# Two plain pairs and a later norm at the head of the squared-relu stages

## The chip, the core and the metric

The kernel runs on one core of a Trainium2 chip. The metric is the device time of one execution, in microseconds (us); less is better. Every execution computes the whole function from inputs in device memory.

## What is computed

Three blocks follow each other on a sequence of 512 tokens with 16 meta tokens in front (528 in all) and a width of 1024: a hybrid layer (gated DeltaNet and short convolution, then a gated MLP), a block of sparse attention, and a block of attention with forget gates ("Fox"). The last two blocks each end with the stage that is changed here. All arithmetic is float32; `w1` of the stage is 1024 x 4096, `w2` 4096 x 1024, `DEPTH_2` is 2.

```python
def rms_norm(x, g):
    xf = x.astype(jnp.float32)
    y = xf * lax.rsqrt(jnp.mean(xf * xf, axis=-1, keepdims=True) + EPS)
    return (y * g.astype(jnp.float32)).astype(x.dtype)

def sq_relu_mlp(x, w1, w2):
    h = jax.nn.relu(x @ w1)
    return (h * h) @ w2
...
    for i in range(DEPTH_2):
        hn = rms_norm(h, attn_norm[i])
...
        h = h + sq_relu_mlp(rms_norm(h, mlp_norm[i]), mlp_w1[i], mlp_w2[i])
    return h[:, N_META:N_META + S]
```

## The kernel before

Activations lie transposed: `h` has 8 tiles of 128 channels by 528 tokens. A float32 product is made of three fp32r matmuls: every operand is split into a high part (ScalarE copies it to fp32r, `xh`, `wh`) and a low part (VectorE subtracts, `xl`, `wl`), and hi x hi, hi x lo and lo x hi are added in PSUM. `products` (line 100) does this for a weight tile of 128 columns that `weight_parts` has split (L83 on ScalarE, L84 on VectorE); weights come through a ring `wr` of three buffers filled by DMAs of the SP queue.

`mlp` runs twice: stage 0 behind the sparse attention on all 528 tokens (halves of 264), stage 1 behind Fox on the last 512 (halves of 256). Its first matrix is cut in 4 chunks of 4 pairs of column tiles. Each pair is multiplied with `seven`, a scheme with seven products of half-size blocks in place of eight: 84 matmuls a pair. For that the weights of a pair are added in four steps (L119 and L120 on VectorE, L121 and L122 on GpSimd) and split (L128, L129); the products are L136. `Squares` combines the results, takes relu and square, and splits them into `fh` and `fl` (L190, L191). After each chunk `down` multiplies with the second matrix (L1032), and `add` multiplies the result by `rrow`, the squared norm factor of each token (L1576), and adds it to `h` (L1577). The channel gains of the norm are in the operands already (`k.par(norm, i)`), the factor of a token comes last, since relu and square let it through as its square.

The token side of `seven` needs seven operands: with the tokens in halves a and b and the channels in halves 1 and 2, these are b11, b21, b22 (scaled parts of `h`) and t1 to t4 (sums of two to four of them). `combined` makes all seven for each of the four channel tiles q, each split in a high part (L1526 or L190) and a low part (L1527 or L191), while `before` still runs the attention's last output projection (L100, residual added at L941). The tiles `xh`/`xl` hold b11, b21, b22 and t3, the tiles `bigh`/`bigl` hold t1, t2 and t4. With `late=True` the first call of `seven` takes the products of b11, b22 and b21 first.

After the second pair, `token_rsqrt` makes the norm's factors: ScalarE squares `h` (L246), GpSimd adds the squares (L247), TensorE sums over channels (L255), VectorE makes the inverse root in a chain of small operations on `rcol` (L215 to L222), TensorE turns `rcol` into a row by five transposes (L266), and L1588 squares it.

The order of instructions on each engine isn't written by hand: the kernel is built with a scheduler that simulates the program and places each operation as its operands and buffers come free. So a change in the code of a stage can move its operations well past those of their neighbours. PSUM has eight banks in one ring (`pd`).

Of the kernel before, what the change touches and what calls it, by code (L numbers as in the profile page):

```python
# [15 lines left out]
D = 1024  # L16
# [30 lines left out]
class K:  # L47
# [56 lines left out]
    def seven(self, wdram, x, n, evac, late=False):  # L104
# [36 lines left out]
        def bank():  # L141
            return self.pst("pd")[:, :half]
# [7 lines left out]
        x1, z = bank(), None  # L150
# [3 lines left out]
        if late:  # L154

            weights(2)
            z = bank()
            product(z, q["s4"], "b22")
            product(x1, q["12"], "b21", start=False)
            evac.out11(x1)  # L160
            weights(1)
        u, y, v = bank(), bank(), bank()
        if late:
            product(y, q["s3"], "t3")
            product(v, q["s1"], "t1")
        product(u, q["s2"], "t2")
        evac.second(u)
        if not late:
            weights(1)
            product(y, q["s3"], "t3")  # L170
            product(v, q["s1"], "t1")
        evac.third(v)
        if not late:
            weights(2)
            product(x1, q["12"], "b21", start=False)
            evac.out11(x1)
        evac.out22(y)
        if not late:
            z = bank()
            product(z, q["s4"], "b22")  # L180
# [1334 lines left out]
def combined(k, h, x, norm, lo, n, pool):  # L1515

    nc = k.nc
    m = n // 2
    a, b = slice(lo, lo + m), slice(lo + m, lo + n)

    def put(name, i, v, scale=None):
        hi, lw = (t[:, i, :m] for t in x[name])
        if scale is None:
            k.split(hi, lw, v)
        else:
            nc.scalar.activation(hi, v, AF.Copy, scale=scale)  # L1526
            nc.vector.scalar_tensor_tensor(lw, v, scale, hi, ALU.mult, ALU.subtract)  # L1527

    for i in range(4):
        p, q = k.par(norm, i), k.par(norm, i + 4)  # L1530
        put("b11", i, h[:, i, a], p)
        put("b21", i, h[:, i + 4, a], q)
        g22 = pool.tile([128, T // 2], F32, name="g22", tag="fh", bufs=RING)[:, :m]
        nc.scalar.activation(g22, h[:, i + 4, b], AF.Copy, scale=q)
        put("b22", i, g22)
        g12 = pool.tile([128, T // 2], F32, name="g12", tag="fh", bufs=RING)[:, :m]
        nc.scalar.activation(g12, h[:, i, b], AF.Copy, scale=p)
        t = pool.tile([128, T // 2], F32, name="gt", tag="fl", bufs=RING)[:, :m]
        nc.vector.tensor_tensor(t, g22, g12, ALU.subtract)
        put("t3", i, t)  # L1540
        t = pool.tile([128, T // 2], F32, name="gt", tag="fl", bufs=RING)[:, :m]
        nc.vector.scalar_tensor_tensor(t, h[:, i, a], p, g12, ALU.mult, ALU.subtract)
        put("t1", i, t)
        nc.vector.tensor_tensor(g22, g22, t, ALU.add)
        put("t2", i, g22, -1.0)
        nc.vector.scalar_tensor_tensor(t, h[:, i + 4, a], q, g22, ALU.mult, ALU.subtract)
        put("t4", i, t, -1.0)


def mlp(k, io, h, i, before, lo=0, n=T):  # L1550
# [3 lines left out]
    w1, w2 = io["wm1"], io["wm2"]  # L1554
    with (
# [6 lines left out]
        pairs = [t[:, 2 * c : 2 * c + 2].rearrange("p a t -> p (a t)").rearrange("p (q t) -> p q t", q=4)  # L1562
                 for t in k.operand2() for c in range(4)]
        x = dict(zip(("b11", "b21", "b22", "t3"), zip(pairs[:4], pairs[4:])))
# [6 lines left out]
        def add(j):  # L1571
# [6 lines left out]

            return ev

        norm = []
# [461 lines left out]
```

## Time and profile before

| | us |
|---|---|
| three runs, median (lowest, highest) | 2635.54 (2629.37, 2642.49) |
| the profiled run, its time | 2630.84 |
| its span | 2629.1 |
| TensorE matmul busy | 2500.4 (95%), 18396 matmuls |
| VectorE busy | 1772.3 (67%) |
| ScalarE busy | 1189.7 (45%) |
| GpSimd busy | 549.3 (21%) |
| mean granted TensorE clock | 0.976 of full |

A busy TensorE isn't yet a TensorE at its peak: a matmul at half clock is busy twice as long. The shares are means over many stages, so the rows further below are taken by stages. In rows of the trace, PE is TensorE's matmuls, PEld its weight loads, DVE VectorE, ACT ScalarE, POOL GpSimd and SPq the queue that issues the DMAs. Lines are those of the kernel before.

### The profile page before, as it was taken

The page shows a single profiled execution, that of the slowest core. Times are in us where ns is not written, and L with a number is a line of the kernel's source. Part 1 is how long each engine was busy: PE and PEld are TensorE (multiplying, and loading weights), DVE is VectorE, ACT ScalarE, POOL GpSimd, SP SyncE. Part 2 cuts the span into 40 slices and gives each one's busy share as a digit, 9 for nine tenths or more (in the row PEclk, how much of TensorE's full clock was granted, in tenths as well). Part 3 has the DMA queues.
Part 4 walks back from the last instruction along what each step waited for, and adds up shares of the span by engine and source line. Part 5 has one row for each costly group of instructions (what it writes and reads, how often), then busy time and mean ns, then how long its engine had stood idle before and what let it go on. Part 6 is the DMA issues. An engine that isn't in the chain of part 4 may idle for free. (4 is left out here: it accounts for less than half of the span.)

```text
span 2629.1 us, 47488 instructions
## 1 busy us (share of the span) xinstructions
PE 2500.4 (95%) x18396; PEld 2315.7 (88%) x18396; DVE 1772.3 (67%) x3698; ACT 1189.7 (45%) x2439; POOL 549.3 (21%) x663
## 2 busy tenths in 40 slices
PE   8899999999999999999869979999999999799999
PEld 8888999999899888888868979999999988688987
DVE  7878788666554444336998496676755777866764
ACT  5434445353423222334447553453535766535533
POOL 2322213100002111013641031121213443211210
PEclk9999999999999999999989989999999989899999
DMA  4334332524562333333321222332433322233322
GB/s 153 92 94 120 84 95 90 118 88 131 171 207 89 96 92 94 96 89 110 83 66 47 72 79 92 105 101 78 129 98 88 90 66 64 66 94 108 105 81 96
DMA packets 148434, 257.32 MB, mean 98 GB/s; under 512 B 66560, under 2 KB 70688, under 8 KB 148208
## 3 DMA queue, kind: packets, MB, share of 16 engines
q1 hardware_dynamic: 91392, 236.47, 29.5%
q10 hardware_dynamic: 56816, 17.82, 3.5%
q8 instruction: 145, 2.38, 0.4%
q14 instruction: 81, 0.66, 0.1%
HBM read 223.39 MB, written 22.34 MB: 93 GB/s over the span
## 5 line engine op out<-in xcount | busy, mean ns | idle before, releaser
L100 PE MATMUL ps_pd<-bigh,wh 128*128 128x256 f32 (+5 forms) x2256 | 693.5, 309 | 16.7 <-ACT bigh L193 6.2
L100 PE MATMUL ps_pd<-bigh,wl 128*128 128x256 f32 (+5 forms) x2256 | 691.4, 308 | 10.5 <-DVE wl L84 10.5
L100 PE MATMUL ps_pd<-bigl,wh 128*128 128x256 f32 (+5 forms) x2256 | 690.6, 307 | 1.8 <-DVE bigl L194 1.5
L83 ACT ACTIVATE wh<-wr 128x1024 fp32r<-128x1024 f32 (+3 forms) x303 | 311.3, 1028 | 657.5 <-PE ps_pd L100 262.0
L100 PEld LDWEIGHTS ps_pd<-bigh,wh 128*128 128x128 f32 (+1 forms) x2256 | 429.5, 191 | 38.0 <-ACT bigh L193 6.2
L100 PEld LDWEIGHTS ps_pd<-bigh,wl 128*128 128x128 f32 (+1 forms) x2256 | 429.6, 191 | 29.9 <-DVE wl L84 12.8
L84 DVE TENSOR_TENSOR wl<-wr,wh 128x1024 fp32r<-128x1024 f32 (+3 forms) x291 | 352.0, 1210 | 152.7 <-ACT wh L83 145.0
L100 PEld LDWEIGHTS ps_pd<-bigl,wh 128*128 128x128 f32 (+1 forms) x2256 | 429.3, 190 | 21.1 <-DVE bigl L194 3.8
L1032 PE MATMUL ps_pd<-fh,wh 128*128 128x264 f32 (+1 forms) x944 | 311.8, 335 | 2.1 <-ACT wh L83 2.1
L1032 PE MATMUL ps_pd<-fl,wh 128*128 128x264 f32 (+1 forms) x944 | 313.5, 334 | 0.0
L1032 PE MATMUL ps_pd<-fh,wl 128*128 128x264 f32 (+1 forms) x944 | 312.1, 335 | 0.5 <-DVE wl L84 0.5
L1032 PEld LDWEIGHTS ps_pd<-fh,wh 128*128 128x128 f32 x944 | 176.2, 188 | 23.1 <-ACT wh L83 4.2
L1032 PEld LDWEIGHTS ps_pd<-fh,wl 128*128 128x128 f32 x944 | 176.7, 188 | 20.0 <-DVE wl L84 1.0
L1032 PEld LDWEIGHTS ps_pd<-fl,wh 128*128 128x128 f32 x944 | 177.1, 188 | 19.1
L128 ACT ACTIVATE wh<-wr 128x1024 fp32r<-128x1024 f32 (+1 forms) x128 | 119.7, 949 | 147.6 <-PE ps_pd L1032 51.2
L129 DVE TENSOR_TENSOR wl<-wr,wh 128x1024 fp32r<-128x1024 f32 (+1 forms) x128 | 154.4, 1219 | 12.3 <-ACT wh L128 11.3
L136 PE MATMUL ps_pd<-xh,wl 128*128 128x264 f32 (+1 forms) x512 | 148.2, 292 | 6.6 <-DVE wl L129 6.4
L136 PE MATMUL ps_pd<-xh,wh 128*128 128x264 f32 (+1 forms) x512 | 149.5, 293 | 3.4 <-ACT wh L128 1.8
L136 PE MATMUL ps_pd<-xl,wh 128*128 128x264 f32 (+1 forms) x512 | 149.0, 291 | 3.4 <-DVE xl L191 2.1
L121 POOL TENSOR_TENSOR wr<-wr 128x512 f32<-128x512 f32 x32 | 51.3, 1602 | 449.8 <-DMA wr<-wm 175.7
L247 POOL TENSOR_TENSOR acc<-acc,sq 128x512 f32<-128x512 f32 (+1 forms) x35 | 60.7, 1735 | 300.4 <-ACT sq L246 300.1
L1576 DVE TENSOR_TENSOR y<-ps_pd,rrow 128x264 f32<-128x264 f32 (+1 forms) x96 | 49.1, 515 | 100.8 <-PE ps_pd L1032 100.7
(501 smaller groups left out, 5527.3 us busy)
## 6 DMA issues: line engine op xcount, KB each, us to landing
wr<-w SPq DMA_DIRECT2D x72, 512.0 KB
wr<-wm SPq DMA_DIRECT2D x128, 256.0 KB
wr<-wm SPq DMA_DIRECT2D x64, 512.0 KB
wr<-wgu SPq DMA_DIRECT2D x44, 512.0 KB
wr<-wa SPq DMA_DIRECT2D x17, 512.0 KB
wr<-wkv SPq DMA_DIRECT2D x17, 512.0 KB
wr<-wdn SPq DMA_DIRECT2D x16, 512.0 KB
wr<-wao SPq DMA_DIRECT2D x16, 512.0 KB
```

The lines of the kernel that those rows point to most:

```text
L83: nc.scalar.activation(wh, wr, AF.Copy)
L84: (self.low or nc.vector).tensor_tensor(wl, wr, wh, ALU.subtract)
L100: nc.tensor.matmul(ps[:, :half], a[:, k], b[k][:, ts], start=(k == 0 and i == 0), stop=(k == kt - 1 and i == 2))
L121: nc.gpsimd.tensor_tensor(g1[:, 1], g2[:, 0], g4[:, 0], ALU.add)
L128: nc.scalar.activation(wh[:, : 4 * m], v, AF.Copy)
L129: nc.vector.tensor_tensor(wl[:, : 4 * m], v, wh[:, : 4 * m], ALU.subtract)
L136: nc.tensor.matmul(ps, a[:, q], c[:, q], start=(start and q == 0 and i == 0), stop=(q == 3 and i == 2), skip_group_check=not start,)
L247: (eng or nc.vector).tensor_tensor(acc, acc, sq, ALU.add)
L1032: nc.tensor.matmul(pss[h][:, :half], a[:, q], b[f0 + q][:, ts], start=(f0 + q == 0 and i == 0), stop=(f0 + q == nf - 1 and i == 2),)
L1576: nc.vector.tensor_tensor(y, ps, rs[:, t], ALU.mult)
```

## The change

The first two pairs of a stage's first chunk (`PLAIN = 2`) are no longer multiplied with `seven` but by `plain`: two weight tiles of 128 columns each, 96 matmuls a pair at L100, with relu, square and split behind each. So the token tiles are now split whole: `xh` and `xl` hold all eight tiles of scaled `h` in 528 (512) columns, and b11, b21, b12 and b22 are views of them. `combined` is replaced by `operand_sums`, which makes t1 to t4 for one channel tile, and is called for two of them behind each plain pair; t3 moves to `bigh`/`bigl`. `seven` loses its `late` order. The squares for the norm are issued behind the first pair that `seven` multiplies, the chain on `rcol` at the end of chunk 0, where `rcol` is squared while it is small, and the five transposes stand in the first call of `add`, at the first result of `down`.

```diff
-    def seven(self, wdram, x, n, evac, late=False):
+    def seven(self, wdram, x, n, evac):
...
-def combined(k, h, x, norm, lo, n, pool):
+def operand_sums(k, h, x, norm, lo, n, i, pool):
...
-    for i in range(4):
-        p, q = k.par(norm, i), k.par(norm, i + 4)
-        put("b11", i, h[:, i, a], p)
-        put("b21", i, h[:, i + 4, a], q)
-        g22 = pool.tile([128, T // 2], F32, name="g22", tag="fh", bufs=RING)[:, :m]
-        nc.scalar.activation(g22, h[:, i + 4, b], AF.Copy, scale=q)
-        put("b22", i, g22)
...
+    g22 = pool.tile([128, T // 2], F32, name="g22", tag="fh", bufs=RING)[:, :m]
+    nc.scalar.activation(g22, h[:, i + 4, b], AF.Copy, scale=q)
+    g12 = pool.tile([128, T // 2], F32, name="g12", tag="fh", bufs=RING)[:, :m]
+    nc.scalar.activation(g12, h[:, i, b], AF.Copy, scale=p)
+    t = pool.tile([128, T // 2], F32, name="gt", tag="fl", bufs=RING)[:, :m]
+    nc.vector.tensor_tensor(t, g22, g12, ALU.subtract)
+    put("t3", t)
...
-        combined(k, h, x, f"mnorm{i}", lo, n, s)
+        for c in (0, 4, 1, 5, 2, 6, 3, 7):
+            k.split(xh[c], xl[c], h[:, c, lo : lo + n], k.par(f"mnorm{i}", c))
+        norm = {}
+
         def add(j):
             def ev(ps, t):
+                if "rs" not in norm:
+                    r = norm["rs"] = p.tile([128, T], F32, name="rrow")
+                    col = norm["col"]
+                    k.rows(
+                        lambda c: col[:, c : c + 1].broadcast_to([CH_DSA[0], 128]), CH_DSA,
+                        lambda ps, t: nc.scalar.activation(r[:, t], ps, AF.Copy),
+                    )
...
+        def plain(w, f):
+
+            for quarters, (fh, fl) in zip(((0, 2), (3, 1)), f):
+                wr = k.wp.tile([128, 8 * 128], F32, name="wr", tag="wr", bufs=k.wr_bufs)
+                wr = wr.rearrange("p (k m) -> p k m", m=128)
+                for e, qt in enumerate(quarters):
+                    nc.sync.dma_start(wr[:, 4 * e : 4 * e + 4], w[:, qt])
+                u = s.tile([128, 2, T], F32, name="u", bufs=2)[:, 0]
+                k.products(k.weight_parts(wr), xh, xl, lambda ps, t: nc.scalar.activation(u[:, t], ps, AF.Relu), n=n)
+                nc.scalar.activation(u[:, :n], u[:, :n], AF.Square)
+                k.split(fh[:, :n], fl[:, :n], u[:, :n])
...
-                k.seven(w1[(i * nf + c * part + j) // 2], x, n, Squares(k, s, n, f[j : j + 2]), c + j == 0)
-                if c == 0 and j == 2:
-                    rs = token_rsqrt(k, p, k.squares(tiles(h), lo=lo, eng=nc.gpsimd))
-                    nc.vector.tensor_tensor(rs, rs, rs, ALU.mult)
-                    norm.append(rs)
+                w = w1[(i * nf + c * part + j) // 2]
+                if c == 0 and j < 2 * PLAIN:
+                    plain(w, f[j : j + 2])
+                    for e in range(4 // PLAIN * (j // 2), 4 // PLAIN * (j // 2 + 1)):
+                        operand_sums(k, h, x, f"mnorm{i}", lo, n, e, s)
+                else:
+                    k.seven(w, x, n, Squares(k, s, n, f[j : j + 2]))
+                if c == 0 and j == 2 * PLAIN:
+                    acc = k.squares(tiles(h), lo=lo, eng=nc.gpsimd)
+            if c == 0:
+                col = norm["col"] = p.tile([CH_DSA[0], 5], F32, name="rcol")
+                k.rsqrt(k.sm, col, k.sumsq(acc, CH_DSA), 1.0 / D, 1e-6, [CH_DSA[0], 5], "rn")
+                nc.vector.tensor_tensor(col, col, col, ALU.mult)
```

The order of instructions of the changed kernel has line numbers of its own; the same operations are L84 (still L84), L926 (was L941), L179 (was L194: the low part of a split with a gain), L176 (was L191), L1017 (was L1032), L251 (was L266), and of the sums L1520, L1523 and L1525 (were L1539, L1542 and L1544). Numbers behind names tell buffers apart; `ps_pd` is a PSUM bank, `params` holds the gains. The first place is VectorE in the out projection of stage 0. Before, the sums of the first channel tile stand between the residuals (`h`) and the projection's weights:

```order
L1527 SCALAR_TENSOR_TENSOR xl_16393<-h_9281,params_77,xh_16392 128x264
L1539 TENSOR_TENSOR gt_16662<-g22_16656,g12_16660 128x264
L1542 SCALAR_TENSOR_TENSOR gt_16666<-h_9281,params_77,g12_16660 128x264
L191 TENSOR_TENSOR xl_16393<-g22_16656,xh_16392 128x264
L941 TENSOR_TENSOR h_9281<-ps_pd_16464,h_9281 128x272
L84 TENSOR_TENSOR wl_16525<-wr_16522,wh_16524 128x1024
L1544 TENSOR_TENSOR g22_16656<-g22_16656,gt_16666 128x264
L191 TENSOR_TENSOR xl_16393<-gt_16662,xh_16392 128x264
```

Changed, from the last residuals of the same projection:

```order
L926 TENSOR_TENSOR h_9281<-ps_pd_16624,h_9281 128x272
L84 TENSOR_TENSOR wl_16752<-wr_16747,wh_16751 128x1024
L179 SCALAR_TENSOR_TENSOR xl_16393<-h_9281,params_77,xh_16392 128x528
L119 TENSOR_TENSOR wr_17013<-wr_17013,wr_17012 128x512
L120 TENSOR_TENSOR wr_17013<-wr_17013,wr_17015 128x512
L84 TENSOR_TENSOR wl_16851<-wr_16846,wh_16850 128x1024
L129 TENSOR_TENSOR wl_17059<-wr_17013,wh_17058 128x1024
L129 TENSOR_TENSOR wl_17124<-wr_17015,wh_17123 128x512
L176 TENSOR_TENSOR fl_16669<-u_16687,fh_16668 128x528
L84 TENSOR_TENSOR wl_16914<-wr_16909,wh_16913 128x1024
L176 TENSOR_TENSOR fl_16671<-u_16750,fh_16670 128x528
L1520 TENSOR_TENSOR gt_16814<-g22_16810,g12_16812 128x264
```

A step of the projection now has one low part of a whole token tile and no sum; the first sums (L1520, L1523) follow the weights of the plain tiles and the first `fl`, behind the projection's end.

The second place is TensorE at the end of the same out projection (matmuls of 272 columns). Before, products of `seven` follow, and soon TensorE goes from bank to bank as operands arrive:

```order
L136 MATMUL ps_pd_16833<-xh_16392,wh_16828 128x264
L136 MATMUL ps_pd_16834<-bigh_16650,wh_16828 128x264
L136 MATMUL ps_pd_16780<-xl_16393,wh_16781 128x264
L136 MATMUL ps_pd_16780<-xh_16392,wl_16782 128x264
L136 MATMUL ps_pd_16832<-bigh_16650,wh_16781 128x264
L136 MATMUL ps_pd_16833<-xl_16393,wh_16828 128x264
L136 MATMUL ps_pd_16833<-xh_16392,wl_16829 128x264
```

Changed:

```order
L100 MATMUL ps_pd_16624<-bigl_14600,wh_16620 128x272
L100 MATMUL ps_pd_16624<-bigh_14599,wl_16621 128x272
L100 MATMUL ps_pd_16692<-xh_16392,wh_16688 128x264
L100 MATMUL ps_pd_16692<-xl_16393,wh_16688 128x264
L100 MATMUL ps_pd_16718<-xh_16392,wh_16688 128x264
L100 MATMUL ps_pd_16718<-xl_16393,wh_16688 128x264
L100 MATMUL ps_pd_16692<-xh_16392,wl_16689 128x264
```

192 matmuls at L100 on `xh` and `xl` stand there, in two halves side by side, before the first L136, and all of them read `xh` and `xl` alone.

The third place is TensorE where the factors of stage 0 are turned into a row (`idn`, `rcol`). Before, they lie between products of the third and fourth pair:

```order
L136 MATMUL ps_pd_16935<-bigl_16651,wh_17015 128x264
L136 MATMUL ps_pd_16935<-bigh_16650,wl_17016 128x264
L266 MATMUL ps_pd_17083<-idn_66,rcol_17060 128x128 x3
L266 MATMUL ps_pd_17088<-idn_66,rcol_17060 128x128
L266 MATMUL ps_pd_17088<-idn_66,rcol_17060 128x16
L136 MATMUL ps_pd_17109<-xh_16392,wh_17110 128x264
L136 MATMUL ps_pd_17109<-xl_16393,wh_17110 128x264
```

Changed, they lie in the first products of `down`:

```order
L1017 MATMUL ps_pd_17328<-fh_16676,wl_17332 128x264
L251 MATMUL ps_pd_17384<-idn_66,rcol_17304 128x128
L1017 MATMUL ps_pd_17327<-fh_16678,wh_17331 128x264
L1017 MATMUL ps_pd_17328<-fh_16678,wh_17331 128x264
L251 MATMUL ps_pd_17384<-idn_66,rcol_17304 128x128 x2
L251 MATMUL ps_pd_17389<-idn_66,rcol_17304 128x128
L251 MATMUL ps_pd_17389<-idn_66,rcol_17304 128x16
L1017 MATMUL ps_pd_17399<-fh_16668,wh_17403 128x264
```

What waited behind them were products of `seven`; now it is a second product of `down`, one transpose being ahead of two of its matmuls.

## Rows read from the trace of the kernel before

**Rows 1.** By stages: busy us (count) per engine, granted clock, DMA share, GB/s

```profile
core 0: us, PE busy (x) PEld busy (x) DVE busy (x) ACT busy (x) POOL busy (x), PEclk, DMA share, GB/s
1505.00:1527.60 22.60, 21.00 (x166) 20.77 (x166) 21.04 (x33) 16.16 (x29) 7.56 (x4) 1.00 0.34 106
1527.60:1570.00 42.40, 30.38 (x186) 26.99 (x184) 37.73 (x66) 23.39 (x46) 14.38 (x9) 0.83 0.16 54
1576.00:1590.00 14.00, 14.00 (x118) 14.00 (x117) 12.18 (x18) 9.43 (x15) 1.46 (x1) 1.00 0.43 140
2100.00:2150.00 50.00, 48.19 (x315) 43.17 (x314) 36.27 (x107) 33.74 (x85) 22.59 (x45) 0.86 0.28 69
2229.70:2252.90 23.20, 18.14 (x72) 13.38 (x73) 19.39 (x34) 14.04 (x32) 6.98 (x6) 0.98 0.25 81
2252.50:2269.00 16.50, 12.94 (x53) 11.37 (x52) 16.50 (x24) 9.73 (x22) 8.00 (x6) 0.50 0.22 72
2252.90:2330.00 77.10, 64.89 (x400) 58.54 (x398) 58.73 (x95) 40.45 (x74) 16.38 (x11) 0.85 0.25 79
```

**Rows 2.** TensorE's waits, 1500 to 1600: us in total, times, longest

```profile
PE ps_pd L266 <- DVE rcol L222: 5.0, 1, 5.0
...
PE ps_pd L100 <- DVE wl L84: 1.6, 1, 1.6
```

**Rows 3.** TensorE's waits, 2225 to 2340

```profile
PE ps_pd L100 <- DVE wl L84: 5.0, 2, 3.9
...
PE ps_pd L266 <- DVE rcol L222: 4.9, 1, 4.9
```

**Rows 4.** TensorE in order of time: start, us, operation [idle before <-releaser]

```profile
1536.69 0.59 PE L136 MATMUL ps_pd<-xh,wl 128*128 128x264 f32 x1 [1.74 <-DVE wl L129]
...
1537.08 0.42 PE L136 MATMUL ps_pd<-xh,wh 128*128 128x264 f32 x1
...
1541.92 0.42 PE L136 MATMUL ps_pd<-xl,wh 128*128 128x264 f32 x1
...
1587.79 0.28 PE L136 MATMUL ps_pd<-xh,wh 128*128 128x264 f32 x1
...
1589.73 0.29 PE L136 MATMUL ps_pd<-xl,wh 128*128 128x264 f32 x1
```

**Rows 5.** TensorE by line, 1527.6 to 1599.7; last row 2252.9 to 2329.4

```profile
L1032 PE MATMUL ps_pd<-fl,wh 128*128 128x264 f32 x22 | 6.0, 285 | 0.0
...
L266 PE MATMUL ps_pd<-idn,rcol 128*128 128x128 f32 (+1 forms) x5 | 1.3, 405 | 5.0 <-DVE rcol L222 5.0
...
L255 PE MATMUL ps_pd<-ones,acc 128*128 128x1 f32 x10 | 1.2, 242 | 0.0
...
L1032 PE MATMUL ps_pd<-fl,wh 128*128 128x512 f32 x16 | 6.3, 395 | 0.0
```

**Rows 6.** VectorE in order of time, stage 0, around the norm's chain

```profile
1563.22 0.69 DVE L120 TENSOR_TENSOR wr<-wr 128x512 f32<-128x512 f32 x1 [1.64 <-DMA wr<-wm]
...
1563.83 1.23 DVE L220 SCALAR_TENSOR_TENSOR rsa<-rsv,rcol 128x5 f32<-128x5 f32 x1
...
1566.94 1.22 DVE L129 TENSOR_TENSOR wl<-wr,wh 128x1024 fp32r<-128x1024 f32 x1
```

**Rows 7.** VectorE in order of time, first and last of seven such rows

```profile
1546.49 0.42 DVE L191 TENSOR_TENSOR xl<-g,xh 128x264 fp32r<-128x264 f32 x1
...
1548.55 0.42 DVE L1527 SCALAR_TENSOR_TENSOR bigl<-gt,bigh 128x264 fp32r<-128x264 f32 x1
```

**Rows 8.** VectorE by shape, whole run: us busy, mean ns

```profile
L194 DVE SCALAR_TENSOR_TENSOR xl<-h,params,xh 128x528 fp32r<-128x528 f32 x8 | 10.3, 1287 | 0.0
...
L194 DVE SCALAR_TENSOR_TENSOR bigl<-xs,params,bigh 128x528 fp32r<-128x528 f32 x8 | 6.8, 864 | 1.5 <-ACT bigh L193 1.5
```

**Rows 9.** GpSimd and VectorE in order of time, stage 0's out projection

```profile
1513.10 1.46 POOL L247 TENSOR_TENSOR acc<-acc,sq 128x528 f32<-128x528 f32 x1 [46.72 <-ACT sq L246]
...
1513.29 1.56 DVE L191 TENSOR_TENSOR xl<-gt,xh 128x264 fp32r<-128x264 f32 x1
```

More of the change, by code (lines that the diff above doesn't have):

```diff
@@ L153, in seven @@
         evac.first(x1)
[L154 to L165, printed above, removed]
         product(u, q["s2"], "t2")
         evac.second(u)
[L168 to L171, printed above, removed]
+        weights(1)
+        product(y, q["s3"], "t3")
+        product(v, q["s1"], "t1")
         evac.third(v)
[L173 to L176, printed above, removed]
+        weights(2)
+        product(x1, q["12"], "b21", start=False)
+        evac.out11(x1)
         evac.out22(y)
-        if not late:
-            z = bank()
-            product(z, q["s4"], "b22")
+        z = bank()
+        product(z, q["s4"], "b22")
         evac.out12(z)
@@ new lines, in operand_sums, with put @@
+    p, q = k.par(norm, i), k.par(norm, i + 4)
+    def put(name, v, sign=1.0):
+        hi, lw = (t[:, i] for t in x[name])
+        nc.scalar.activation(hi, v, AF.Copy, scale=sign)
+        if sign == 1.0:
+            nc.vector.tensor_tensor(lw, v, hi, ALU.subtract)
+        else:
+            nc.vector.scalar_tensor_tensor(lw, v, sign, hi, ALU.mult, ALU.subtract)
+    g22 = pool.tile([128, T // 2], F32, name="g22", tag="fh", bufs=RING)[:, :m]
+    nc.scalar.activation(g22, h[:, i + 4, b], AF.Copy, scale=q)
@@ new lines, in operand_sums @@
+    g12 = pool.tile([128, T // 2], F32, name="g12", tag="fh", bufs=RING)[:, :m]
[3 more added lines that the diff above has]
+    put("t3", t)
+    t = pool.tile([128, T // 2], F32, name="gt", tag="fl", bufs=RING)[:, :m]
+    nc.vector.scalar_tensor_tensor(t, h[:, i, a], p, g12, ALU.mult, ALU.subtract)
+    put("t1", t)
+    nc.vector.tensor_tensor(g22, g22, t, ALU.add)
@@ L1561, in mlp @@
         k.wq = wq
-        pairs = [t[:, 2 * c : 2 * c + 2].rearrange("p a t -> p (a t)").rearrange("p (q t) -> p q t", q=4)
-                 for t in k.operand2() for c in range(4)]
-        x = dict(zip(("b11", "b21", "b22", "t3"), zip(pairs[:4], pairs[4:])))
+        big2 = k.operand2()
+        xh, xl = ([t[:, :n] for t in tiles(x)] for x in big2)
         before((0, 4, 1, 5, 2, 6, 3, 7))
-        pairs = [t[:, 2 * c : 2 * c + 2].rearrange("p a t -> p (a t)").rearrange("p (q t) -> p q t", q=4)
-                 for t in k.operand() for c in range(3)]
@@ L1568, in mlp @@
-        x.update(zip(("t1", "t2", "t4"), zip(pairs[:3], pairs[3:])))
-        combined(k, h, x, f"mnorm{i}", lo, n, s)
-        x = {c: tuple(t[:, :, : n // 2] for t in v) for c, v in x.items()}
+        x = {
+            c: tuple(t[:, r : r + 4, o : o + m] for t in big2)
+            for c, r, o in (("b11", 0, 0), ("b21", 4, 0), ("b12", 0, m), ("b22", 4, m))
+        }
+        big = k.operand()
+        for c, name in enumerate(("t1", "t2", "t3", "t4")):
+            x[name] = tuple(
+                t[:, 2 * c : 2 * c + 2].rearrange("p a t -> p (a t)").rearrange("p (q t) -> p q t", q=4)[:, :, :m] for t in big
+            )
```

30 lines of the change are left out of this document (8 added, 22 removed).

## Prediction, made before the changed kernel was run

> **What bounds the kernel now.** I read the table by stages first, then what TensorE waited for in two of the stages, then the order of time there. By stages TensorE is full in the steady part (1576 to 1590: 14.00 of 14.00 us) and not full at the head of either squared-relu stage: 30.38 of 42.40 us at a granted clock of 0.83, and 64.89 of 77.10 at 0.85 [rows 1]. VectorE is nearly full in the same places (37.73 of 42.40; 16.50 of 16.50 between 2252.5 and 2269). So each stage's head is bound by VectorE, not by products. The waits say on what: on `rcol` of the norm 5.0 and 4.9 us, and else on weight parts (`wl`) that VectorE writes late, 1.6 and 5.0 in the out projections alone [rows 2, 3]. The third loss is the clock: after a run of such gaps, the last of 1.74 us, matmuls of 264 columns start every 0.220 us (22 steps in 4.84), where the full pitch is 0.121 (16 steps in 1.94) [rows 4]. The granted clock is 1.00 at the full pitch and 0.50 in the like stretch of stage 1, 2252.5 to 2269 [rows 1]: 2.4 and 1.2 GHz.
>
> How much is lost. Stage 0, from the first L136 to the first use of `rrow`, 1527.6 to 1599.7: 72.1 us. At full pitch its work is 4 pairs of 84 matmuls, 336 x 0.121 = 40.7, three times 21 or 22 of the down products [rows 5] at the same pitch 7.9, and 2.5 for the norm's sums and turns [rows 5]: 51.1. Lost: 21.0, and 1.6 at a gap of the out projection ahead of it [rows 2]. Stage 1, 2252.9 to 2329.4, 76.5 us: 336 x 0.1175 (0.121 x 256/264, an estimate) = 39.5, three times 15 or 16 down matmuls [rows 5] of 512 columns at 0.235 (scaled in the same way) = 11.0, 2.5 as before: 53.0, lost 23.5. Its out projection takes 23.2 us [rows 1] for 72 matmuls of 512 columns, 16.9: lost 6.3. Together 52.4 us.
>
> **The change part by part.** *Plain pairs.* A pair costs 96 matmuls in place of 84: 24 more a stage, 2.9 and 2.8 us, 5.7 in all. This is certain and on the path: where TensorE waits for nothing, nothing hides it.
>
> *VectorE, per stage.* Gone: two pairs' preparation, each with L119 and L120, three `wl` of 1024 and one of 512 columns and five evacuations (0.69 x 2 + 3 x 1.22 + 0.69 + 5 x 0.42 = 7.8, so 15.6 undisturbed [rows 6, 7]), and the twelve `lo` of b11, b21 and b22, 0.42 or more each. Added: four `wl` at L84 (1.22 each) and eight `xl` of 528 columns; in the Fox attention, beside GpSimd's squares, those took 1.29 each, and the same shape elsewhere 0.86 [rows 8], so 7 to 10 us. The balance is about -9, with bounds from -12 to -4. What matters more: the 32 operations for t1 to t4, 0.42 each and 0.343 from start to start (6 steps in 2.06 [rows 7]), today stand in front of the first products or between them; now they lie under 192 matmuls that need only `xh` and `xl`, 23.2 us. In these 23.2 us VectorE has 32 x 0.36 = 11.5 for sums (some are a little longer), two `wl` of L84, two of L129, two pairs of L119 and L120 and four `fl`: some 21.5. That is close to full, so I followed both engines by hand from the end of the out projection. TensorE reaches a product with the last two quarters of t after the 192 and 54 more (on views of `xh` and on quarters 0 and 1), at 29.8. VectorE, with three or four operations stretched beside GpSimd as today [rows 9] and one wait of 1.6 for a weight transfer [rows 6], ends the last sums near 35. They are taken up one by one, so this leaves some 2 us of waiting, 0 to 8.
>
> *The first product.* It needs all eight tiles of `xh` and `xl`, but one by one in the order of the matmuls: tile 7 is asked for 21 matmuls (2.5 us) after the first, and its `lo` follows the last residual by a `wl` (1.2) and its own 0.9. I take 0.5 us a stage. In stage 0's out projection VectorE has a residual (some 0.4), a `wl` (1.2) and an `xl` (0.9) for each 24 matmuls of 3.0 us: covered, and the gap of 1.6 goes, unless every step meets a square on GpSimd. In stage 1 VectorE is busy 19.4 of the 23.2 us [rows 1]; eleven operations of the sums leave it (11 x 0.42 and 1.1 for one that GpSimd holds), and the fourth quarter's `lo` comes in (1.6): 15.3 of 16.9, with little room. Of the 6.3 I leave 4.
>
> *The norm.* The five turns leave the middle of the pairs for the first `add`, and the squares start behind the first seven-product pair. The chain of small operations was late since it stood behind a wait for a transfer (1.64) and one link on 5 columns took 1.23 [rows 6]. By the same hand count `rcol` is ready at 46 and asked for at 49. So the waits of 5.0 and 4.9 go, and the turns' own 1.3 stays. Should that cover of 3 us fail, further down products stand ready in the other PSUM banks, so it costs little.
>
> *Queues.* SP issues 14 transfers fewer a stage; the plain weights come through the same ring of three buffers. GpSimd loses four sums of weights a stage, and its seven squares stand ahead of the first L121 now.
>
> *The sum.* Left in stage 0: 2 for sums, 0.5 at the start, 1.5 for weights. Left in stage 1: the same, 4 in the out projection, and 1 since its matmuls are shorter. 52.4 - 5.7 - 4 - 9 = 33.7 us. The second half of the Fox attention is put in another order with the same operations; its clock (0.86 over 2100 to 2150 [rows 1], 7 us) can move either way: 0, from -7 to +7. The profiled run took 2630.84 us (span 2629.1), and the median of the three is 4.7 above it. 33.7 off the run is 2597.1, off the median 2601.8. What is measured is a median, so I say **2602**, and for this case 2587 to 2615.
>
> **Rivals.** *Late sums.* VectorE's 21.5 of 23.2 us leave 1.7 for GpSimd. A `lo` of 0.42 that met a square took 1.56 and ended 0.3 after it [rows 9]: 1.1 for each meeting. With all seven squares and the first weight sums there (11 meetings, 12 us) the first seven-product pair waits some 8 us and starts at the low clock: 8 + 84 x 0.099 = 16 a stage in place of 4. Gain 33.7 less 20 to 24: 2622 to 2626. Behind the row stands a rule of the Trainium skill (SBUF — State Buffer, "Who interferes with whom"): a VectorE instruction with two inputs in SBUF and a GpSimd instruction that reads SBUF lock each other out for the whole instruction. The rows agree, and by it each of the 32 sums is open to this. Against it: the squares come behind the first seven-product pair in the program, and today they are spread over both parts.
>
> *Nothing gained.* The waits only move: the 6.3 us in stage 1's out projection stay, the `wl` of the first seven-product pair is late by a transfer (3 us) with 4 at the low clock behind it in each stage, and Fox is 7 longer. 33.7 - 2.3 - 2 x 7 - 7 = 10: 2625.
>
> *Slower.* The low clock takes the plain products: if the eight `xl` starve TensorE, the 192 matmuls run at 0.220 in place of 0.121, 19 us a stage, 38. It decides once gaps like that of 1.74 us [rows 4] stand ahead of the first plain product and the level stays to the end of the sums. 33.7 - 38 - 5 for one more wait on sums in stage 1: 9 slower, 2645, or 2652 with Fox against it. Against it: in stage 0 the clock is 1.00 up to 1527.6 [rows 1], and a plain product needs one new weight tile per 48 matmuls (5.8 us), where VectorE's share is 1.2. For it: 0.50 over 16.5 us of stage 1.
>
> *Not what it says.* That the sums don't lie under the plain products is excluded by the order shown.
>
> **How the numbers follow.** Forecast 0.68; better than 2587 (nothing left in either stage, Fox faster) 0.06; late sums 0.13; nothing gained 0.08; slower 0.05. The range leaves out the best and the worst tenth: 2586 to 2623. A measurement of this kernel can tell about 0.5% (13 us) from no change, so faster means under 2622.4: 0.68 + 0.06 + most of late sums' near half and a little of the next, 0.84; within 0.5% 0.12; slower 0.04.
>
> **What would show it.** Right: no wait on `rcol`; 192 matmuls at L100 on `xh` and `xl` in 23 to 24 us at clock 1.00; from the first plain product to the first `y` 58 us in stage 0 and 61 in stage 1. Wrong: waits of the first L136 on `bigl` of over 8 us, a clock near 0.5 under the plain products, over 3 us of gaps in stage 0's out projection, or a Fox attention whose length moves by over 7 us.

## The result and the profile after

The changed kernel took 2596.52 us in the median of four runs (2593.67 to 2599.42) against 2635.03 of the kernel before, measured again with it (2629.37 to 2642.49): a ratio of 0.985, with a 95% interval of 0.983 to 0.988, 38.5 us less. Forecast were 2602, 33 less. The profiled run of the changed kernel took 2599.42 us (span 2597.7).

Engine totals, from the page of the changed kernel:

```profile
PE 2494.6 (96%) x18444; PEld 2315.0 (89%) x18444; DVE 1740.6 (67%) x3654; ACT 1182.2 (46%) x2423; POOL 543.2 (21%) x655
```

TensorE has 48 matmuls more and is busy 6 us less: behind the out projections it no longer runs at a lowered clock (0.83 and 0.85 in [rows 1], 1.00 in the rows below). The stages of the changed kernel, to be held against [rows 1] (three windows for each stage: out projection, plain products, then up to the first `y`; the columns are the same):

```profile
1505.40:1531.30 25.90, 25.83 (x193) 25.83 (x193) 16.35 (x22) 14.48 (x19) 4.28 (x3) 0.93 0.43 144
1531.30:1554.70 23.40, 23.40 (x195) 23.40 (x194) 20.18 (x23) 16.88 (x32) 14.52 (x8) 1.00 0.24 79
1554.70:1588.20 33.50, 31.49 (x247) 30.02 (x247) 27.25 (x62) 22.55 (x44) 2.52 (x1) 1.00 0.33 103
2221.20:2239.00 17.80, 17.24 (x72) 13.38 (x73) 13.82 (x22) 11.02 (x19) 4.10 (x3) 1.00 0.41 133
2239.00:2262.00 23.00, 22.92 (x188) 22.36 (x187) 20.54 (x22) 16.66 (x32) 12.71 (x8) 1.00 0.29 97
2262.00:2298.60 36.60, 34.11 (x234) 30.68 (x233) 27.98 (x65) 22.71 (x47) 2.42 (x1) 1.00 0.31 94
```

TensorE is full and at full clock under the plain products, and nearly so behind them; VectorE is busy 20 of the 23 us under the plain products. What TensorE waited for in stage 0, 1505 to 1590 (against [rows 2]), and in stage 1, 2221 to 2300 (against [rows 3]):

```profile
PE ps_pd L136 <- DVE wl L129: 0.7, 2, 0.4
PE ps_pd L100 <- DVE bigl L176: 0.7, 1, 0.7
PE ps_pd L136 <- ACT wh L128: 0.7, 1, 0.7
PE ps_pd L136 <- DVE bigl L1511: 0.6, 1, 0.6
```

```profile
PE ps_pd L100 <- DVE o L1870: 0.9, 1, 0.9
PE ps_pd L136 <- ACT wh L128: 0.7, 1, 0.7
PE ps_pd L136 <- DVE wl L129: 0.6, 1, 0.6
PE ps_pd L136 <- DVE bigl L1511: 0.6, 1, 0.6
PE ps_pd L100 <- DVE wl L84: 0.5, 1, 0.5
...
PE ps_pd L136 <- ACT bigh L1509: 0.2, 1, 0.2
```

No wait on `rcol` is left, and none above 1 us. I call a stage's *head* the stretch from the first matmul of its out projection to its first `y` (the first result of `down` times the norm's factor). Both heads together fell from 199.4 us (27.7 + 72.0 and 23.2 + 76.5) to 160.0 (25.8 + 56.9 and 17.7 + 59.6), 39.4 less. In the two profiled runs the rest of the program was 8.0 us longer in the run of the changed kernel, 5.5 of it ahead of the first head, where nothing was changed. Of the 39.4 us, 7.4 lie in the two out projections (50.9 to 43.5).

### The profile page after: what moved, and what is told of

It reads as the page before. It is cut to its first block, busy times and chain, and to the rows that moved or that the text cites. A ratio compares the mean times of both kernels' runs of the same rounds, so it can differ in the third digit from the quotient of the medians.

```text
span 2597.7 us, 47491 instructions
## 1 busy us (share of the span) xinstructions
PE 2494.6 (96%) x18444; PEld 2315.0 (89%) x18444; DVE 1740.6 (67%) x3654; ACT 1182.2 (46%) x2423; POOL 543.2 (21%) x655
## 5 line engine op out<-in xcount | busy, mean ns | idle before, releaser
L100 PE MATMUL ps_pd<-bigh,wh 128*128 128x256 f32 (+5 forms) x2256 | 695.3, 310 | 18.3 <-ACT bigh L178 6.6
L100 PE MATMUL ps_pd<-bigh,wl 128*128 128x256 f32 (+5 forms) x2256 | 692.3, 308 | 3.3 <-DVE wl L84 3.3
L100 PE MATMUL ps_pd<-bigl,wh 128*128 128x256 f32 (+5 forms) x2256 | 692.4, 308 | 1.4 <-DVE bigl L179 1.2
L83 ACT ACTIVATE wh<-wr 128x1024 fp32r<-128x1024 f32 (+3 forms) x311 | 319.7, 1029 | 666.6 <-PE ps_pd L100 264.3
L84 DVE TENSOR_TENSOR wl<-wr,wh 128x1024 fp32r<-128x1024 f32 (+3 forms) x299 | 365.8, 1224 | 156.6 <-ACT wh L83 149.1
L100 PEld LDWEIGHTS ps_pd<-bigh,wh 128*128 128x128 f32 (+1 forms) x2256 | 430.9, 191 | 40.3 <-ACT bigh L178 7.0
L100 PEld LDWEIGHTS ps_pd<-bigh,wl 128*128 128x128 f32 (+1 forms) x2256 | 430.6, 191 | 21.5 <-DVE wl L84 4.4
L100 PEld LDWEIGHTS ps_pd<-bigl,wh 128*128 128x128 f32 (+1 forms) x2256 | 430.5, 191 | 20.8 <-DVE bigl L179 3.4
L1017 PE MATMUL ps_pd<-fh,wh 128*128 128x264 f32 (+1 forms) x944 | 312.2, 335 | 1.8 <-ACT wh L83 1.8
L1017 PE MATMUL ps_pd<-fl,wh 128*128 128x264 f32 (+1 forms) x944 | 313.3, 335 | 0.0
L1017 PE MATMUL ps_pd<-fh,wl 128*128 128x264 f32 (+1 forms) x944 | 312.2, 335 | 0.0
L1017 PEld LDWEIGHTS ps_pd<-fh,wh 128*128 128x128 f32 x944 | 176.4, 188 | 22.4 <-ACT wh L83 3.5
L1017 PEld LDWEIGHTS ps_pd<-fl,wh 128*128 128x128 f32 x944 | 177.1, 188 | 19.1
L1017 PEld LDWEIGHTS ps_pd<-fh,wl 128*128 128x128 f32 x944 | 176.7, 188 | 19.0
L128 ACT ACTIVATE wh<-wr 128x1024 fp32r<-128x1024 f32 x112 | 105.1, 950 | 135.4 <-PE ps_pd L1017 55.8
L129 DVE TENSOR_TENSOR wl<-wr,wh 128x1024 fp32r<-128x1024 f32 x112 | 135.4, 1221 | 11.7 <-ACT wh L128 10.9
L136 PE MATMUL ps_pd<-bigh,wh 128*128 128x264 f32 (+1 forms) x448 | 125.8, 285 | 6.2 <-DVE u L1480 4.6
L121 POOL TENSOR_TENSOR wr<-wr 128x512 f32<-128x512 f32 x28 | 45.6, 1627 | 403.3 <-DVE wr L119 154.3
L136 PE MATMUL ps_pd<-bigl,wh 128*128 128x264 f32 (+1 forms) x448 | 125.1, 283 | 1.2 <-DVE bigl L1511 1.2
L136 PE MATMUL ps_pd<-bigh,wl 128*128 128x264 f32 (+1 forms) x448 | 123.8, 282 | 0.0
```

What stands on the lines that cost most here:

```text
L83: nc.scalar.activation(wh, wr, AF.Copy)
L84: (self.low or nc.vector).tensor_tensor(wl, wr, wh, ALU.subtract)
L100: nc.tensor.matmul(ps[:, :half], a[:, k], b[k][:, ts], start=(k == 0 and i == 0), stop=(k == kt - 1 and i == 2))
L121: nc.gpsimd.tensor_tensor(g1[:, 1], g2[:, 0], g4[:, 0], ALU.add)
L128: nc.scalar.activation(wh[:, : 4 * m], v, AF.Copy)
L129: nc.vector.tensor_tensor(wl[:, : 4 * m], v, wh[:, : 4 * m], ALU.subtract)
```

## Experiments

The question was which part of the change brought this. Beside the times stands the length of both heads in the run's profile. Each ratio is to the kernel before as it was measured beside that run (medians of 2632.89 to 2635.03 us). The heads aren't quite alike: ahead of the first `y` stand 63 and 44 matmuls of `down` in the changed kernel, 65 and 47 before, 59 and 26 with four plain pairs, 51 and 33 with four and the chain early. At 0.121 and 0.23 us each, the heads of the two kernels with four pairs hold some 4 to 5 us less work than the changed kernel's for that reason alone.

| kernel | median, us | ratio to before (95%) | both heads, us |
|---|---|---|---|
| before | 2635.03 | 1 | 199.4 |
| changed | 2596.52 | 0.985 (0.983 to 0.988) | 160.0 |
| norm alone moved | 2632.04 | 1.000 (0.998 to 1.001) | 195.0 |
| changed, norm in its old place | 2623.49 | 0.995 (0.993 to 0.997) | 182.9 |
| changed, turns alone late | 2593.63 | 0.986 (0.984 to 0.988) | 160.5 |
| before without sums | 2632.12 | 1.000 (0.999 to 1.001) | 196.0 |
| norm moved, without sums | 2603.54 | 0.990 (0.987 to 0.993) | 171.3 |
| changed, sums first | 2610.63 | 0.992 (0.989 to 0.994) | 168.5 |
| changed, one plain pair | 2623.84 | 0.996 (0.995 to 0.998) | 185.9 |
| one plain pair, `late` order | 2623.02 | 0.997 (0.995 to 0.998) | 182.7 |
| two plain pairs, `late` order | 2597.51 | 0.988 (0.985 to 0.991) | 161.3 |
| four plain pairs | 2594.93 | 0.986 (0.984 to 0.989) | 156.4 |
| changed, one square | 2596.51 | 0.987 (0.984 to 0.989) | 158.6 |
| four plain pairs, chain early | 2591.01 | 0.984 (0.982 to 0.986) | 155.4 |

**The norm alone.** In the kernel before, squares and chain go behind the third pair and the turns into `add`:

```diff
-                if c == 0 and j == 2:
-                    rs = token_rsqrt(k, p, k.squares(tiles(h), lo=lo, eng=nc.gpsimd))
+                if c == 0 and j == 4:
+                    acc = k.squares(tiles(h), lo=lo, eng=nc.gpsimd)
```

> The kernel before with the norm alone moved as in the change (squares behind the third pair, the chain at the end of chunk 0, the turns in the first add); all four pairs still by seven products, the token operands still made in front. Theory A (VectorE is late at the head of each stage because of the token sums; the norm's wait is a part of its own): the waits of 5.0 and 4.9 us on rcol go, and with them the stretch at half clock behind each (about 1.5 us a stage): 9 to 13 us faster than before, 2622 to 2626; out projections and first products wait as before. Rival B (the norm's wait is the main loss): 20 us or more faster, 2615 or less. Rival C (the wait only moves to the weight parts behind it): under 4 us.

No difference that can be measured: rival C. TensorE's longest waits in this run's stage 0, 1504 to 1604:

```profile
PE ps_pd L136 <- DVE wl L129: 3.5, 4, 1.7
PE ps_pd L136 <- ACT wh L128: 3.3, 2, 2.8
PE ps_pd L100 <- DVE wl L84: 1.6, 1, 1.6
```

The 5.0 us on `rcol` [rows 2] are gone, and 2.8 on a weight part stand where they stood: both waits come behind 168 products of `seven`. That is two pairs, so in the kernel before the turns stand in front of the third pair, and not between the third and the fourth as the section on the change has it. Both heads together are 4.4 us shorter, not 9 to 13.

**Plain pairs with the norm in its old place.** The changed kernel with `token_rsqrt`, turns and all, behind the second pair:

```diff
-                if c == 0 and j == 2 * PLAIN:
-                    acc = k.squares(tiles(h), lo=lo, eng=nc.gpsimd)
+                if c == 0 and j == 2:
+                    rs = token_rsqrt(k, p, k.squares(tiles(h), lo=lo, eng=nc.gpsimd))
```

> The changed kernel with the norm in its old place: squares, chain and turns behind the second (plain) pair, in front of the first seven products. A: the wait on rcol is back with 4 to 8 us a stage, since VectorE has the last sums to make there, and some of it at half clock: 8 to 16 us slower than the changed kernel, 2605 to 2613. B: 20 us slower or more. C: within 4 us of the changed kernel.

27 us slower than the changed kernel (22.9 in the heads): my theory gave 8 to 16, and the size is rival B's. But B as a whole had just failed with the norm alone. TensorE's longest wait in stage 0, 1500 to 1595; the first and the last links of the chain with two between, in order of time on VectorE; then the split of the first weights of `seven` on VectorE and the first product of `seven` on TensorE:

```profile
PE ps_pd L251 <- DVE rcol L207: 12.7, 1, 12.7
```

```profile
1552.40 0.15 DVE L200 TENSOR_SCALAR rsv<-ps_pd 128x5 f32<-128x5 f32 x1
1553.60 1.25 DVE L201 TENSOR_SCALAR rst<-rsv 128x5 int32<-128x5 int32 x1
...
1559.24 0.16 DVE L205 SCALAR_TENSOR_TENSOR rsa<-rsv,rcol 128x5 f32<-128x5 f32 x1
...
1562.34 0.17 DVE L207 SCALAR_TENSOR_TENSOR rcol<-rsa,rcol 128x5 f32<-128x5 f32 x1
```

```profile
1535.43 2.92 DVE L129 TENSOR_TENSOR wl<-wr,wh 128x1024 fp32r<-128x1024 f32 x2
...
1563.82 0.59 PE L136 MATMUL ps_pd<-xh,wh 128*128 128x264 f32 x1
```

TensorE comes to the turns right behind the plain products and stands there 12.7 us. The products of `seven` come behind the turns in its queue and wait with them: the first has its weights split at 1538.4 and starts at 1563.82, while in the changed kernel, without turns there, it starts 0.1 us behind the last plain product. The chain's twelve links take some 0.16 us each (one 1.25), but between them stand token sums on VectorE's queue, so the chain takes 10 us. Stage 1 has the same with 13.0 us.

**The turns alone.** The changed kernel, with squares and chain left in that old place, and the turns late:

```diff
-                if c == 0 and j == 2 * PLAIN:
+                if c == 0 and j == 2:
                     acc = k.squares(tiles(h), lo=lo, eng=nc.gpsimd)
-            if c == 0:
-                col = norm["col"] = p.tile([CH_DSA[0], 5], F32, name="rcol")
+                    col = norm["col"] = p.tile([CH_DSA[0], 5], F32, name="rcol")
```

> The changed kernel with squares and chain in their old place (behind the second plain pair), and only the five turns left in the first add. Theory T (what cost 27 us with the whole norm in its old place is that TensorE, in order, stands at the turns until the chain is through): within 4 us of the changed kernel, no wait of TensorE on rcol. Rival Q (the chain's small operations between the sums hold VectorE back): 10 us or more slower than the changed kernel.

2593.63, no wait on `rcol` and none above 0.9 us: theory T. The 27 us came from where the five transposes stand in TensorE's queue (their copies and the square of the row move with them); where the chain and GpSimd's squares stand costs nothing that the medians show.

**Sums left out.** Now the other half: the kernel before, and the same with the norm moved, without the 32 sum operations of a stage.

```diff
-        t = pool.tile([128, T // 2], F32, name="gt", tag="fl", bufs=RING)[:, :m]
-        nc.vector.tensor_tensor(t, g22, g12, ALU.subtract)
-        put("t3", i, t)
...
+        x.update(t1=x["b11"], t2=x["b21"], t3=x["b22"], t4=x["b11"])
```

> The kernel before with the 32 sum operations of each stage (and their ScalarE copies) left out: t1 to t4 are views of b11, b21 and b22, so the result is not the reference's. All pairs by seven products, the norm where it was. Measures what the sums cost the kernel before. Theory A2 (two things in series hold the head: VectorE's sums, and behind them TensorE at the turns): the sums' part goes, but the turns still stand in front of the third pair: 10 to 25 us faster than before, 2609 to 2624, a wait on rcol of 3 to 10 us a stage left. Rival B2 (the weights of the seven products alone fill VectorE): under 8 us faster.

> The same without sums, and the norm moved as in the change; the pairs are all by seven products. The result is not the reference's. A2: with both gone the head is full but for the weights: 5.7 us less work than the changed kernel, some waits on weight parts more: 2586 to 2598, level with the changed kernel or a little faster. Rival B2: 2610 or more, with waits on wl of L129 and half clock, so that plain pairs help by their lighter weights and not by covering sums.

The first is as slow as before, against theory and near the rival's number, but not for the rival's reason: with the norm moved as well, 29 us go. Waits of stage 0 in the first (1500 to 1600) and in the second (1494 to 1585):

```profile
PE ps_pd L266 <- DVE rcol L222: 12.5, 1, 12.5
PE ps_pd L136 <- DVE wl L129: 2.9, 1, 2.9
```

```profile
PE ps_pd L136 <- ACT wh L128: 3.4, 2, 2.9
PE ps_pd L136 <- DVE wl L129: 3.3, 2, 2.9
PE ps_pd L100 <- DVE wl L84: 2.0, 1, 2.0
```

Without sums TensorE is at the turns 27.1 us behind the out projection in place of 36.1, but `rcol` is ready only at 39.6 in place of 41.0: between the chain's links VectorE now has splits of weights and of results. So TensorE waits 12.5 us there in place of 5.0. The other gate is VectorE, in the first 24 us behind the out projection of stage 0, with the norm moved, with the sums and without them (columns as in the stages above):

```profile
1532.30:1556.00 23.70, 16.67 (x83) 13.89 (x82) 23.70 (x34) 13.61 (x30) 11.41 (x7) 0.80 0.14 46
```

```profile
1523.20:1547.00 23.80, 20.40 (x153) 19.96 (x152) 18.48 (x23) 11.04 (x19) 10.27 (x7) 0.93 0.24 78
```

With sums VectorE is busy all of the time and TensorE gets 83 matmuls done, at a mean clock of 0.80; without them it does 153. So two gates stood one behind the other, VectorE's sums and the turns, and either alone hid what the other was worth: without the sums both heads together were 3.4 us shorter (199.4 to 196.0), with the norm moved 4.4 (195.0), with both 28.1 (171.3). And the second kernel, with no sums at all and 5.7 us fewer products, is still 7 us behind the changed one, 11.3 in the heads. Of these, 6.9 lie in the out projections (28.1 and 22.3 us in place of 25.8 and 17.7), where no plain product stands: there the split of whole token tiles, which this kernel lacks, is what differs, and in stage 1 the clock (0.93 and 1.00). Behind them its waits are on weights of the first seven-product pairs, so that part of the rival is right: plain weights are lighter for VectorE. No run has the whole token tiles without plain pairs, so how the two share these 11.3 us is only argued.

**Where the sums stand.** All four calls of `operand_sums` ahead of the plain pairs:

```diff
+        for e in range(4):
+            operand_sums(k, h, x, f"mnorm{i}", lo, n, e, s)
         norm = {}
```

> The changed kernel with all operand sums in front of the two plain pairs in the program, so that the scheduler may take them before the plain weights and splits. A (it is the place of the sums that counts, not their number): if they go into the out projection again, first products are late by 5 to 9 us a stage: 2606 to 2615, with gaps in the out projection. Rival C (less VectorE work for weights is what counts, wherever the sums stand): within 4 us of the changed kernel.

14 us slower than the changed kernel (8.5 in the heads), as theory A has it, but by another engine. The out projection has no gap in stage 0; TensorE waits under the plain products (1500 to 1590), and in stage 1 in the same way, 3.9 us:

```profile
PE ps_pd L100 <- ACT wh L83: 7.2, 2, 6.7
```

On ScalarE the high parts of the sums stand ahead of the plain weights' split (L83), and wait for VectorE one by one. The clock falls with the longer wait: it was 1.00 from the end of the out projection up to it, and is 0.50 over the 4 us behind it:

```profile
1543.46:1547.50 4.04, 3.47 (x14) 3.16 (x15) 3.99 (x7) 4.04 (x10) 0.00 (x0) 0.50 0.58 169
```

**How many plain pairs.** One in place of two; one with the `late` order of the first seven-product pair put back; and four, with squares and chain behind the fourth:

```diff
-PLAIN = 2
+PLAIN = 1
```

> The changed kernel with one plain pair instead of two; all four operand sums behind it. Two times 12 matmuls fewer (2.9 us for both stages). A (the sums need the cover of both pairs): the cover is 11.6 us and 6.5 for products on the views, VectorE ends the sums 10 us or more later than asked for, with half clock behind it: 8 to 20 us slower than the changed kernel, 2605 to 2617. Rival D (the gain is the whole token tiles and the norm; one pair's cover is enough): 1 to 4 us faster than the changed kernel.

```diff
-                    k.seven(w, x, n, Squares(k, s, n, f[j : j + 2]))
+                    k.seven(w, x, n, Squares(k, s, n, f[j : j + 2]), c == 0 and j == 2 * PLAIN)
...
-PLAIN = 2
+PLAIN = 1
```

> One plain pair and the removed order (b11, b22, b21 first) in the first seven-product pair behind it: 11.6 + 4.4 us of products without t. With one plain pair and the other order, TensorE waited 4.5 and 5.5 us on a weight part and 2.6 on a sum. If the sums were what is late, the order takes 2 to 6 us of it: 2616 to 2622; if the weights of the first seven-product pair are late, it changes nothing or asks for the third group too early: 2622 to 2630.

```diff
-                if c == 0 and j == 2 * PLAIN:
+                if c == 0 and j == 6:
...
-PLAIN = 2
+PLAIN = 4
```

> The changed kernel with four plain pairs in the first chunk (one channel tile's sums behind each, squares behind the fourth, first seven-product pair in chunk 1). It measures the price of a plain pair where nothing waits any more: 48 more matmuls in both stages, 5.7 us, less what is left of the waits on sums and weights (2 to 3 us a stage). Theory A: 1 to 5 us slower than the changed kernel. Rival M (VectorE is still the bound of the whole chunk, so more plain pairs help): 3 us or more faster.

One pair is not enough. Its longest waits in stage 0 (1499 to 1596):

```profile
PE ps_pd L136 <- DVE wl L129: 4.5, 1, 4.5
PE ps_pd L136 <- ACT wh L128: 2.7, 1, 2.7
PE ps_pd L136 <- ACT bigh L1509: 2.6, 1, 2.6
```

Two of the three are weights, and the `late` order, which puts off the sums alone, changes nothing: medians of 2623.02 against 2623.84, and TensorE idle for 24.1 against 24.0 us behind the out projections. Four pairs are not slower than two (2594.93), though they bring 5.7 us of products; their shorter heads (156.4) are no gain, since 22 matmuls of `down` fewer stand in them. What is left to wait for is `rcol`, in stage 0 (1500 to 1584) and stage 1 (2219 to 2295):

```profile
PE ps_pd L251 <- DVE rcol L1603: 0.3, 1, 0.3
...
PE ps_pd L251 <- DVE rcol L1603: 2.2, 1, 2.2
```

With two pairs the `late` order (the first of the two edits of the run with one pair) changes nothing either:

> The changed kernel with the removed order of the first seven-product pair put back (products of b11, b22, b21 first, which need only views of xh and xl): 24 more matmuls, 2.9 us, stand in front of the first use of t. Theory A (waits on the sums are 1 to 2 us a stage): 1 to 3 us faster than the changed kernel, or the same. Rival W (that order asks for the third weight group first, which comes later): 2 to 5 us slower, with a wait on a weight part of that group.

2597.51 against 2596.52: no difference.

**GpSimd's squares.** The changed kernel with the square of one tile in place of all eight:

```diff
-                    acc = k.squares(tiles(h), lo=lo, eng=nc.gpsimd)
+                    acc = k.squares(tiles(h)[:1], lo=lo, eng=nc.gpsimd)
```

> The changed kernel with one square of h in place of eight (seven GpSimd additions and seven ScalarE squares a stage are left out, so the norm's factors are those of one channel tile). In the changed kernel GpSimd is busy 12.9 of the 23.3 us of the plain products, and eight VectorE operations there take 1.1 us longer. Theory A (that is covered now): within 3 us of the changed kernel, the waits of 0.6 and 0.7 us shorter at most. Rival L (the lock costs time still): 4 to 8 us faster.

2596.51: no difference in the medians (2589.42 to 2599.81 in four runs, so 2 us would not show). GpSimd is busy 4.31 us under the plain products of stage 0 here, and 14.52 with all squares (the expectation had 12.9), and VectorE 16.65 in place of 20.18:

```profile
1524.30:1547.70 23.40, 23.40 (x195) 23.40 (x194) 16.65 (x23) 14.94 (x29) 4.31 (x3) 1.00 0.26 79
```

**Both free edits together.** Four plain pairs, with the edit of the run with the turns alone late (squares and chain behind the second pair):

```diff
-PLAIN = 2
+PLAIN = 4
```

> Four plain pairs, with squares and chain behind the second of them and the turns in the first add: the two edits that cost nothing by themselves, together. With four plain pairs and the chain behind them, TensorE still waited 0.3 and 2.2 us on rcol. If that wait is on the path it goes: 2 to 3 us faster than with four pairs alone, 2591 to 2594, the fastest so far by a hair. If not: 2594 to 2597, the same as the changed kernel, and the head has nothing left to give.

2591.01 (2587.87 to 2597.19), 0.984 with 0.982 to 0.986: the fastest median, with no wait of TensorE in either stage behind its out projection. But its interval overlaps that of the changed kernel (0.983 to 0.988), so 5 us between them are not shown.

## Where the prediction was right and where not

Direction and size held: 38.5 us came for 33 forecast, the time lies in the range (2586 to 2623) and in the likeliest case's own (2587 to 2615). Of the mechanism, the signs held (no wait on `rcol`, plain products at full clock, both heads near their forecast); where the sums lie and how the waits add up was told wrongly. By the terms of the sum, from the profiled runs:

| term | predicted, us | measured, us |
|---|---|---|
| plain products of stage 0 at clock 1.00 | 23 to 24 | 23.3 |
| first plain product to first `y`, stage 0 | 58 | 56.9 |
| the same, stage 1 | 61 | 59.6 |
| out projection of stage 1 | 20.9 | 17.7 |
| last sum ended, from the first plain product, stage 0 | 35 | 38.4 |
| of 32 sums a stage, started under the plain products | 32 | 8 |
| waits on sums, a stage | 2 (0 to 8) | 0.6 and 0.8 |
| `rcol` ready / asked for, stage 0 | 46 / 49 | 48.6 / 52.2 |
| Fox attention, from the last product of stage 0 | 0 (-7 to +7) | +2.6 |

The times of `rcol` and of the last sum are these rows, against the first plain product at 1531.30 (VectorE, then the turns on TensorE):

```profile
1568.94 0.77 DVE L1513 SCALAR_TENSOR_TENSOR bigl<-gt,bigh 128x264 fp32r<-128x264 f32 x2
...
1579.78 0.17 DVE L1603 TENSOR_TENSOR rcol<-rcol 128x5 f32<-128x5 f32 x1
```

```profile
1583.49 0.27 PE L251 MATMUL ps_pd<-idn,rcol 128*128 128x128 f32 x1
```

*The term that was mis-sized* is the 4 us left in stage 1's out projection, where 0.8 stayed (17.7 against 16.9 of products). I had VectorE busy for 15.3 us there and saw little room; it is busy 13.82 of 17.80, and TensorE waits 0.5 us on a weight part. That is 3.2 of the 5.7 us by which the heads gained more than the sum. About half of it is luck: in five other kernels with plain pairs the same stretch with the same waits took 19.1 to 19.3 us at a clock of 0.91 or 0.92 (a row is shown at the end). The rest is about 1 us in each head.

*The sum was right as a whole and wrong by its parts.* I measured what both heads lost against full pitch, and that total was a sound base. But I told it as if the waits were its terms ("so the waits of 5.0 and 4.9 go"). Runs show they are not: moving the norm is worth nothing in the kernel before and 27 us with plain pairs in front, and the sums are worth nothing while the turns stand in their place. Had the change moved only the norm, the same reading would have given some 10 us where none came; my expectation for that run, 9 to 13, made just this mistake. The norm's part also had that a late `rcol` would cost little, since products in other banks stand ready behind the turns. They don't go ahead of the turns: with the norm in its old place TensorE stood there 12.7 and 13.0 us.

*"Certain and on the path": 5.7 us for 24 more matmuls a stage.* The matmuls are on the path (192 in 23.3 us). That they cost 5.7 was too sure: 48 more with four pairs show no loss in the median. TensorE's idle time in the heads is 1.9 us less there (4.6 to 2.7); what makes up for the rest isn't shown, and a loss of 1 or 2 us is below what a median shows.

*Not what it says.* The prediction excluded "by the order shown" that the sums don't lie under the plain products. Yet only 8 of the 32 start there, in either stage. The first sum of stage 0 starts 16.4 us behind the first plain product, after the splits of weights and of `fl`, and the other 24 run beside the first products of `seven`, while VectorE is busy all of the time:

```profile
1547.67 0.42 DVE L1520 TENSOR_TENSOR gt<-g,g 128x264 f32<-128x264 f32 x1
```

```profile
1554.70:1569.70 15.00, 12.99 (x95) 11.72 (x95) 14.99 (x30) 11.48 (x25) 2.52 (x1) 1.00 0.26 79
```

The order of one engine doesn't say how far another engine is by then. TensorE waited 0.6 us on sums all the same, since the first products of `seven` take views of `xh` and the quarters of t as they come, as the forecast's count had it. This suggests that the plain pairs help by needing no sums and only light weights, more than by having the sums under them: with the sums first, all 32 start before the last plain product, and that kernel is 14 us slower.

*Late sums.* The rival's place was real, and half of my argument against it was wrong: the squares come behind in the program, yet the scheduler takes five of their seven additions to the start of the plain products, and GpSimd is busy 14.52 of 23.40 us there:

```profile
1530.76 9.60 POOL L232 TENSOR_TENSOR acc<-acc,sq 128x528 f32<-128x528 f32 x5 [4.20 <-ACT sq L231]
...
1558.61 2.52 POOL L122 TENSOR_TENSOR wr<-wr 128x512 f32<-128x512 f32 x1 [6.66 <-DVE bigl L1513]
```

The trace agrees with the Trainium skill (SBUF — State Buffer, "Who interferes with whom"): a split of 0.70 us on VectorE met the second of these rows and took 1.71:

```profile
1559.99 1.71 DVE L176 TENSOR_TENSOR fl<-u,fh 128x528 fp32r<-128x528 f32 x1
```

The last sum of stage 0 came 3.4 us later than I had it, but the squares aren't the reason: with one square it ended 38.2 us behind the first plain product in place of 38.4, though VectorE was busy 3.5 us less under the plain products. What VectorE waited for from the first plain product to the last sum, with all squares and with one:

```profile
DVE wr L119 <- DMA wr<-wm: 2.5, 2, 1.3
DVE wl L84 <- ACT wh L83: 0.6, 1, 0.6
```

```profile
DVE wr L119 <- DMA wr<-wm: 4.2, 2, 2.4
DVE wl L84 <- ACT wh L83: 2.4, 3, 1.3
```

Where GpSimd holds VectorE less, VectorE waits longer for the same weights: the two additions of weights at L119 start 5.4 and 18.5 us behind the first plain product with all squares, 5.5 and 18.3 with one. So the longer operations filled time that was lost to transfers in any case. In stage 1 the last sum did come 2.0 us sooner with one square (36.9 in place of 38.9), which the medians can't tell.

*Queues.* SP doesn't issue fewer transfers, as I had it: both kernels issue 828, 192 of them for the weights of the two stages. The sum had no term for it.

*Nothing gained, slower.* Neither came: the clock was 1.00 from the first plain product on in both stages. The slower rival rested on half clock under the plain products. That came only with the sums first, behind a wait of 6.7 us, and that kernel was still 22 us faster than before. With the norm in its old place the clock fell behind the plain products (0.90 over the stage, 1525.4 to 1593.4), with one plain pair too (0.88).

## What to carry to other kernels

Two waits that stand one behind the other on an engine that goes by its queue have no prices of their own: here taking away either one gave nothing, and both together 29 us. So sum up what a stretch loses against its full pitch, and ask of each edit what the engine meets next, in the queue's order. A few tiny instructions that need a late result (here five transposes) held TensorE for 12 us in which, without them, it makes products; put them where their result is used, not where it could be had. And an order of instructions on one engine shows what stands behind what there, not what another engine is doing at the time: for that, put both on one clock.

## What was not expected

The same stretch of program isn't equally long in each execution: in the profiled runs above, the first head began between 1494.8 and 1505.5 us, though every engine has the same instructions ahead of it, in the same order but for four small matmuls. From the first head's end to the second's start went 630.0 to 639.8 us; there the scheduler's order differs between most kernels, so this shows less. So a single profile can't tell 5 us of a whole run. How well the heads repeat for one and the same kernel isn't shown, since each has one profile.

The out projection of stage 0 took 25.8 us in the changed kernel and 24.3 with the norm in its old place, with the same 193 matmuls and the same idle of 0.7 us ahead. The difference is the clock alone, 0.93 and 1.00 over the stretch. Here is that stretch in the latter kernel; the changed one's is the first row of its stages above:

```profile
1501.10:1525.40 24.30, 24.30 (x193) 24.30 (x194) 16.35 (x21) 14.49 (x19) 4.30 (x3) 1.00 0.49 153
```

The out projection of stage 1 does the same: 17.7 us at 1.00 in the changed kernel, 19.3 at 0.91 with the norm in its old place.

```profile
2225.90:2245.20 19.30, 18.83 (x73) 14.55 (x74) 13.85 (x21) 11.00 (x19) 4.07 (x3) 0.91 0.37 122
```

What decides which of the two comes stays open; no run was made for it. It puts 1.5 us of chance on each stage's head in the table of the experiments.
